# Thirteen buffers in place of ten for a stream of expert weights, a new order of the last chunks, and earlier stores

## The chip, the cores and the metric

The kernel runs on one core of a Trainium2 chip. Its time is the device time of one execution in microseconds (us); of several executions the median is taken. TensorE (PE) multiplies matrices, VectorE (DVE), ScalarE (ACT) and GpSimd (POOL) work element by element, SyncE (SP) here only issues loads and stores, which 16 DMA engines carry out.

## The reference

Two layers of a diffusion transformer act on 256 latent tokens (and, in the first, on 256 context tokens) of width 1024. Layer 0 mixes by neighbourhood attention and a convolution and has a dense feed-forward part. Layer 1 mixes by a state-space model, and its feed-forward part is a mixture of eight experts, each token going to two of them. The change concerns this last part:

```
def moe_swiglu(h, w_router, w1, w3, w2):
    t = h.reshape(-1, shp[-1])
    logits = _f32(t @ w_router)
    top_val, top_idx = lax.top_k(logits, TOP_K)
    top_w = jax.nn.softmax(top_val, axis=-1)
    gate = jnp.einsum('tk,tke->te', top_w, jax.nn.one_hot(top_idx, N_EXPERTS, ...))
    out = gate[:, 0:1] * swiglu(t, w1[0], w3[0], w2[0])
    for e in range(1, N_EXPERTS):
        out = out + gate[:, e:e + 1] * swiglu(t, w1[e], w3[e], w2[e])
```

with `swiglu(h, w1, w3, w2) = (silu(h @ w1) * (h @ w3)) @ w2`, an inner width of 3584, and all weights in 32-bit floating point. The experts' weights are 8 x 3 x 1024 x 3584 numbers, 352 MB, and each is used once. Everything is multiplied in full 32-bit precision or in the three-product split described below.

## The kernel before

**Places for tokens.** After routing, the experts are sorted by how many tokens they got. Eight places are compiled: places 0, 3 and 6 are large, with 128 slots, places 1, 2, 4, 5 and 7 are small, with 64 (`FEW`). Place 0 is always expert 0, so that its weights can be loaded before the routing is known; the others read their expert's number from a register on SyncE (`values_load` in `moe`). If a place overflows, `overflow` runs a slow path behind a test of a counter, which all engines make; with these inputs it isn't taken.

**Chunks and units.** An expert's inner width is cut into seven chunks of 512. A chunk needs six units of weights, each 128 x 2048 numbers, 1 MB: two of w1 (`m1`), two of w3 (`m3`), two of w2 (`m2`). One step of `moe` does the up products of one chunk (`m1`, `m3`) and then the down product (`m2`) of the chunk of the step before.

- A *large* chunk uses units that were split into a high and a low part: ScalarE casts each half of a unit (`wh`, line 203) and VectorE subtracts (`wl`, line 205; GpSimd does it for the names in `ON_POOL`). TensorE then makes three products (`mm3`, lines 223 to 225): 72 matmuls of 512 columns a chunk. A split unit's buffer is free as soon as the split is done. The parts go to a ring of pairs; `need` splits the unit in use and the next two, if they belong to large chunks.
- A *small* chunk uses its units as they are: `up_few` (line 2024) and the small branch of `down` (line 2058), 48 matmuls a chunk, two at a time on two halves of the array. Its buffers are free when the products have read them.

**The ring of loads.** `Stream` keeps a list of free buffers and a list of units in order of use (`mseq`). Every release issues the next unit's load on SyncE's queue, which takes its issues in order; so the order of releases in the program fixes which release a load waits for. The ring has ten buffers in the experts' part: four of its own (`raw`) and six that were lent: one in `xres`, one in `h`, two in `U`, two in `room`. The queue also keeps no more than eight loads under way.

**The pairs.** In the experts' part there are six pairs of split halves: four of the ring (`wh`, `wl`) and two in a tile `more`. During the routing (the end of `s5`) the first three units of expert 0 are split ahead, the third by VectorE (first half) and GpSimd (second half).

**The order of the steps.** `moe_plan` puts three large chunks first and then mixes the other 18 large with the 35 small ones in proportion. Its last steps are the small chunks 4 and 5 of place 7, the last large chunk, the last small chunk. TensorE, ScalarE, GpSimd and SyncE run in the order in which the code is written; VectorE's order is chosen by the scheduler.

**The end.** After an expert's seventh chunk its output is multiplied by the gate of the second residual (`g2row`), scattered back by matmuls with a permutation (`scatter`, `scatter_few`) and added to the residual stream (`added`, line 1923). Each of these six actions of an expert is spread over later steps, one at a time (`ADDS`). At the very end comes the overflow test and then four stores of the result (`full`, line 2187).

Of the kernel before, what the change touches and what calls it, by code (L numbers as in the profile page):

```python
# [156 lines left out]
class Kernel:  # L157
# [1077 lines left out]
    def s5(self, xT):  # L1235
# [218 lines left out]
        gate, self.g2row = gates[:, 0], gates[:, 1]  # L1454
        self.kept(0, gate)
# [118 lines left out]
        first = self.mseq[:3]  # L1574
# [37 lines left out]
        self.split(first[2])  # L1612
# [8 lines left out]
        room = up.tile([P, 2, UNIT], F32, name="room", tag="y")  # L1621
        self.st.lend(room[:, 0], room[:, 1])
# [345 lines left out]
    def moe_plan(self):  # L1968

        many, few = ([(e, c) for e in range(8) if FEW[e] == i for c in range(7)] for i in range(2))  # L1970
        self.steps = many[:LAG]
        del many[:LAG]
        while many or few:
            self.steps.append((many if len(many) * 7 * sum(FEW) > len(few) * (7 * (8 - sum(FEW)) - LAG) else few).pop(0))
        seq, last = [], []
        for e, c in self.steps:
            seq += [(k, e, c, j) for j in range(2) for k in ("m1", "m3")] if FEW[e] else \
                   [(k, e, c, j) for k in ("m1", "m3") for j in range(2)]
            seq += last
            last = [("m2", e, c, j) for j in range(2)]  # L1980
        seq += last
        for s in seq:
            self.st.add(s, partial(self.moe_src, *s))
        self.mseq = seq
        self.expert = {}
# [7 lines left out]
    def moe(self):  # L1993
# [4 lines left out]
        def need(name):  # L1998
            i = pos[name]
            for j in (i, i + 1, i + 2):  # L2000
                if j < len(seq) and not FEW[seq[j][1]]:
                    self.split(seq[j])
# [67 lines left out]
        few = self.hT.rearrange("p k t -> p (k t)")[:, 0:1024].rearrange("p (a b) -> p a b", a=2)  # L2070
# [8 lines left out]
        def finish(e, c, t):  # L2079
# [3 lines left out]
            if c == 6:  # L2083
# [3 lines left out]
                adds.extend([acts[i] for i in v] for v in ADDS)  # L2087
# [45 lines left out]
        while adds:  # L2133
            step()

    def overflow(self):
# [3 lines left out]
        with tc.If(most > 0):  # L2140
            for e in range(8):
                n = nc.values_load(self.cnt[0:1, e:e + 1], min_val=0, max_val=256)
                with tc.If(n > 0):
# [34 lines left out]
                    for n in range(2):  # L2178
                        ready(n)
                        add(n)  # L2180

    def full(self):
        self.layer0()
        for n in range(2):
            for t in range(2):
                s = slice(n * 512, n * 512 + 512)
                self.nc.sync.dma_start(self.out[0, t * P:(t + 1) * P, s], self.x[:, 2 + t, s])
# [100 lines left out]
ADDS = ((0,), (1,), (2,), (3,), (4,), (5,))  # L2288
TAIL = (0, 0, 2, 0, 1, 1)
# [7 lines left out]
LAG = 3  # L2297

# [29 lines left out]
```

## Time and profile before

| what | us |
|---|---|
| median of 3 executions | 1849.68 (1848.10 to 1851.54) |
| profiled execution, its time | 1849.28 |
| profiled execution, its span (first to last instruction) | 1847.5 |
| TensorE busy in the span | 1690.4 (91%) |
| VectorE, ScalarE, GpSimd busy | 1144.5, 719.8, 475.3 |
| loads and stores in the span | 517.03 MB |
| mean granted TensorE clock | 0.962 of 2.4 GHz |

The busy shares are averages over many stages with different limits; a change to one stage is read from that stage. Times in the trace count from the start of the span. TensorE's matmuls overlap, and their ends are modelled, so a busy TensorE is not one at its peak. The DMA share is the mean busy share of the 16 DMA engines (values a little over 1 are rounding of the recorder), GB/s what they moved. "PEclk" is the clock granted to TensorE, as a share of the full 2.4 GHz; 0.50 is the lower level of 1.2 GHz.

### The profile page before, as it was taken

Reading aid. Unit: us, or ns where it says so; the run is one execution under the profiler, and the core shown is the slowest. Engines: PE = TensorE matmul, PEld = TensorE weight load, DVE = VectorE, ACT = ScalarE, POOL = GpSimd, SP = SyncE. Lnnn points to the kernel's source line nnn. Section 1 sums busy time; section 2 is a strip of 40 time slices with the busy share of each in tenths; the row PEclk is TensorE's granted clock in tenths of the full one; section 3 lists DMA queues with packets and bytes.
Section 4 is the critical chain, followed back from the end, with each engine's and each line's share of the span. In section 5 each row is a group of like instructions: output and inputs, shape, how many; then the busy total and the mean of one; then the engine's idle time right before and its main releaser. Section 6 shows DMA issues by size and latency. Waiting matters only on the chain.

```text
span 1847.5 us, 23203 instructions
## 1 busy us (share of the span) xinstructions
PE 1690.4 (91%) x8562; PEld 1122.3 (61%) x8562; DVE 1144.5 (62%) x1614; ACT 719.8 (39%) x1069; POOL 475.3 (26%) x541
## 2 busy tenths in 40 slices
PE   6967899998988999998689999989999999999997
PEld 4855366876766778665567755544544564554553
DVE  4999788577576664669969654454444444445444
ACT  3435563432332332457265533333333332333331
POOL 2347038396695720152432000000000000000000
PEclk9988899999999999999698999999999998999999
DMA  8320743664653653357966899999999999999995
GB/s 320 126 83 23 245 154 139 211 217 145 226 177 119 215 185 114 144 179 142 290 275 232 327 421 420 419 420 420 419 420 420 420 419 398 404 419 421 419 420 225
DMA packets 107432, 517.03 MB, mean 280 GB/s; under 512 B 13792, under 2 KB 41696, under 8 KB 48688
## 3 DMA queue, kind: packets, MB, share of 16 engines
q1 hardware_dynamic: 76672, 490.77, 69.0%
q10 hardware_dynamic: 29968, 22.57, 3.8%
q0 software_dynamic: 672, 2.14, 0.4%
q8 instruction: 69, 1.13, 0.2%
q14 instruction: 51, 0.42, 0.1%
HBM read 496.46 MB, written 18.97 MB: 279 GB/s over the span
## 4 chain that ended last, share of the span: by engine, by line
PE 43%; DMA 12%; DVE 7%; POOL 2%; ACT 1%; issue 1%; SPq 0%; ACTq 0%; DVEq 0%; POOLq 0%
PE m L2024 10%; PE y L2058 5%; DMA U<-in_moe 4%; PE m L223 3%; PE m L224 3%; PE m L225 3%; DMA room<-in_moe 3%; PE w L223 2%; PE w L225 2%; PE w L224 2%; DMA raw<-in_moe 2%; PE y L224 2%; PE y L223 2%; PE y L225 2%; DVE wl L205 1%
## 5 line engine op out<-in xcount | busy, mean ns | idle before, releaser
L205 DVE TENSOR_TENSOR wl<-raw,wh 128x1024 fp32r<-128x1024 f32 x151 | 192.4, 1309 | 93.2 <-ACT wh L203 93.2
L203 ACT CAST wh<-raw 128x1024 fp32r<-128x1024 f32 x172 | 173.6, 1048 | 172.2 <-PE w L225 73.9
L2024 PE MATMUL m<-raw,E 128*64 128x512 f32 x456 | 178.2, 597 | 0.0
L224 PE MATMUL w<-hl,wh 128*128 128x512 f32 (+1 forms) x384 | 143.6, 374 | 1.2 <-POOL hl L568 0.6
L223 PE MATMUL w<-hh,wh 128*128 128x512 f32 (+1 forms) x384 | 144.4, 377 | 0.0
L225 PE MATMUL w<-hh,wl 128*128 128x512 f32 (+1 forms) x384 | 142.4, 372 | 0.0
L1845 POOL TENSOR_SCALAR brow<-order 128x128 fp32r<-128x128 f32 x10 | 9.3, 941 | 473.9 <-PE bk L1880 462.4
L224 PE MATMUL m<-wl,small 128*128 128x512 f32 x252 | 100.9, 401 | 9.7 <-DVE wl L205 9.7
L223 PE MATMUL m<-wh,small 128*128 128x512 f32 x252 | 101.6, 403 | 4.8 <-ACT wh L203 4.8
L2024 PE MATMUL m<-U,E 128*64 128x512 f32 x232 | 105.4, 597 | 0.0
L225 PE MATMUL m<-wh,small 128*128 128x512 f32 x252 | 100.0, 397 | 0.0
L2046 ACT CAST small<-gT 128x512 fp32r<-128x512 f32 x21 | 12.3, 586 | 221.8 <-PE gT L2043 221.8
L2047 DVE TENSOR_TENSOR small<-gT,small 128x512 fp32r<-128x512 f32 x21 | 14.5, 692 | 131.8 <-ACT small L2046 131.8
L2024 PE MATMUL m<-room,E 128*64 128x512 f32 x208 | 94.4, 597 | 0.0
L2024 PEld LDWEIGHTS m<-raw,E 128*64 128x64 f32 x456 | 51.1, 136 | 60.9 <-issue 58.6
L223 PEld LDWEIGHTS w<-hh,wh 128*128 128x128 f32 x384 | 72.2, 188 | 16.7 <-issue 3.6
L224 PEld LDWEIGHTS w<-hl,wh 128*128 128x128 f32 x384 | 72.3, 188 | 14.8 <-POOL hl L568 2.8
L224 PE MATMUL w<-wl,gh 128*128 128x512 f32 x176 | 71.8, 408 | 10.4 <-DVE wl L205 10.4
L225 PEld LDWEIGHTS w<-hh,wl 128*128 128x128 f32 x384 | 72.2, 188 | 12.9
L205 POOL TENSOR_TENSOR wl<-raw,wh 128x1024 fp32r<-128x1024 f32 x21 | 52.7, 2521 | 98.0 <-ACT wh L203 98.0
L2040 ACT COPY E<-gT 128x256 f32<-128x256 f32 x35 | 13.0, 371 | 160.1 <-PE gT L2038 160.1
L223 PE MATMUL w<-wh,gh 128*128 128x512 f32 x176 | 71.6, 407 | 1.9 <-ACT wh L203 1.9
(444 smaller groups left out, 4270.6 us busy)
## 6 DMA issues: line engine op xcount, KB each, us to landing
raw<-in_moe SPq DMA_DIRECT2D x135, 1024.0 KB, 15.5
U<-in_moe SPq DMA_DIRECT2D x67, 1024.0 KB, 15.6
room<-in_moe SPq DMA_DIRECT2D x66, 1024.0 KB, 13.1
raw<-in_ada_w SPq DMA_DIRECT2D x48, 1024.0 KB, 5.3
xres<-in_moe SPq DMA_DIRECT2D x34, 1024.0 KB, 16.4
h<-in_moe SPq DMA_DIRECT2D x34, 1024.0 KB, 17.1
raw<-in_ffn_w SPq DMA_DIRECT2D x30, 1024.0 KB, 5.1
raw<-in_mix_w_in SPq DMA_DIRECT2D x10, 1024.0 KB, 6.5
```

The costliest lines, as they stand in the source:

```text
L203: nc.scalar.copy(wh[:, :m], flat[:, h:h + m])
L205: eng.tensor_tensor(wl[:, :m], flat[:, h:h + m], wh[:, :m].bitcast(F32), op=OP.subtract)
L223: nc.tensor.matmul(o, lhsT=ah, rhs=bh, start=start, stop=False)
L224: nc.tensor.matmul(o, lhsT=ah, rhs=bl, start=False, stop=False)
L225: nc.tensor.matmul(o, lhsT=al, rhs=bh, start=False, stop=stop)
L1845: eng.tensor_scalar(self.perm[:, int(FEW[e]), t], self.iota64 if FEW[e] and not beyond else self.iota, pos, mask, op0=OP.is_equal, op1=OP. ...
L2024: nc.tensor.matmul(o[64 * i:64 * i + 64], lhsT=self.few[:, 4 * j + k], rhs=w[i][:, k], start=not j and not k, stop=j == 1 and k == 3, tile ...
L2040: nc.scalar.copy(gT, pt[:, 0:256])
L2046: nc.scalar.copy(gh, v)
L2047: nc.vector.tensor_tensor(gl, v, gh.bitcast(F32), op=OP.subtract)
L2058: nc.tensor.matmul(y[64 * n:64 * n + 64], lhsT=t[:, 2 * j + f], rhs=w[:, f, n * 512:n * 512 + 512], start=not c and not j and not f, stop= ...
```

## The change

- The ring has 13 buffers, not 10. New are the tile `E[0]` (which held the transposed tokens for routing and then the small experts' inputs and hidden values) and two units in a new tile `more`, in the place of the two split pairs. The small experts' inputs and hidden values move to the tile of the first residual's gate, which is spent by then (`self.spent`).
- Four split pairs remain, so `need` splits the unit in use and only the next one, and the routing splits two units ahead, not three; the third is split in the first step of the experts.
- The order of steps ends with four small chunks: the last three (`LAST`) are kept back when large and small ones are mixed.
- A small expert's six actions at its end are taken in three steps (`FEW_ADDS`).
- The four stores are issued straight after the last addition, ahead of the overflow test; the overflow path stores again if it runs.

```diff
+        self.spent = gate
...
-        first = self.mseq[:3]
+        first = self.mseq[:2]
         self.split(first[0])
...
-        self.split(first[2])
...
         room = up.tile([P, 2, UNIT], F32, name="room", tag="y")
         self.st.lend(room[:, 0], room[:, 1])
+        self.st.lend(E[0].rearrange("p a b c -> p (a b c)"))
+        self.rings = [self.ring_pair]
+        room = up.tile([P, 2, UNIT], F32, name="more", tag="L1")
+        self.st.lend(room[:, 0], room[:, 1])
...
+        n, m = len(many), len(few) - LAST
         while many or few:
-            self.steps.append((many if len(many) * 7 * sum(FEW) > len(few) * (7 * (8 - sum(FEW)) - LAG) else few).pop(0))
+            self.steps.append((many if many and len(many) * m > (len(few) - LAST) * n else few).pop(0))
...
-            for j in (i, i + 1, i + 2):
+            for j in (i, i + 1):
                 if j < len(seq) and not FEW[seq[j][1]]:
                     self.split(seq[j])
...
-        few = self.hT.rearrange("p k t -> p (k t)")[:, 0:1024].rearrange("p (a b) -> p a b", a=2)
+        few = self.spent.rearrange("p (a b) -> p a b", a=2)
...
-                adds.extend([acts[i] for i in v] for v in ADDS)
+                adds.extend([acts[i] for i in v] for v in (FEW_ADDS if FEW[e] else ADDS))
...
         while adds:
             step()
+        self.store()
+
+    def store(self):
+        for t in range(2):
+            for n in range(2):
+                s = slice(n * 512, n * 512 + 512)
+                self.nc.sync.dma_start(self.out[0, t * P:(t + 1) * P, s], self.x[:, 2 + t, s])
...
                     for n in range(2):
                         ready(n)
                         add(n)
+            self.store()
 
     def full(self):
         self.layer0()
-        for n in range(2):
-            for t in range(2):
-                s = slice(n * 512, n * 512 + 512)
-                self.nc.sync.dma_start(self.out[0, t * P:(t + 1) * P, s], self.x[:, 2 + t, s])
...
+FEW_ADDS = ((0, 1), (2, 4), (3, 5))
...
+LAST = 3
```

The order of the steps (L a large chunk, s a small one) was

`L L L s L s L s s L s s L s s L s s L s s L s s L s s L s s L s s L s s L s s L s s L s s L s s L s s L s`

and is now

`L L L s L s L s s L s s L s s L s L s s L s s L s s L s s L s L s s L s s L s s L s L s s L s s L s s L s s s s`

Three places in the engines' orders follow. First SyncE's queue at the end of the routing; the loads are named by the buffer that they fill, and `TENSOR_LOAD cnt` reads the first expert's number. Before:

```order
L85 DMA raw<-in_moe 128x2048 x2
L85 DMA xres<-in_moe 128x2048
L85 DMA raw<-in_moe 128x2048
L85 DMA room<-in_moe 128x2048 x2
L85 DMA h_7842<-in_moe 128x2048
L2104 TENSOR_LOAD cnt
```

The same place in the changed kernel:

```order
L85 DMA raw<-in_moe 128x2048 x2
L85 DMA xres<-in_moe 128x2048
L85 DMA room<-in_moe 128x2048 x2
L85 DMA E_7049<-in_moe 128x2048
L85 DMA more<-in_moe 128x2048 x2
L85 DMA raw<-in_moe 128x2048
L2109 TENSOR_LOAD cnt
```

Two loads more stand ahead of the numbers' reading, and the load into a `raw` buffer that waited for the third split now stands behind the lent tiles.

Second, VectorE at the same place (the names: `pw` holds the routing's small tables, `brow` the selection matrix of the first place, `h` the tokens that are selected). Before, from the ranks of the second half of the tokens on:

```order
L1766 TENSOR_REDUCE pw<-gt 128x8
L1767 TENSOR_SCALAR pw<-pw 128x8
L205 TENSOR_TENSOR more<-raw,more 128x1024
L1752 SCALAR_TENSOR_TENSOR h_7842<-T_7536,rn 128x512 x2
L1781 COPY pw<-pos 128x8
```

and in the changed kernel:

```order
L1770 TENSOR_REDUCE pw<-gt 128x8
L1771 TENSOR_SCALAR pw<-pw 128x8
L1756 SCALAR_TENSOR_TENSOR h_7842<-T_7536,rn 128x512 x2
L1785 COPY pw<-pos 128x8
L1795 TENSOR_SCALAR pw<-pw 128x16
```

The split's subtraction (line 205) has left this place; it stands in the first step of the experts.

Third, VectorE at the end of the program (`m` is a chunk's hidden part, `y` an expert's output, `sc` a scattered part, `xres` the residual). Before:

```order
L2047 TENSOR_TENSOR small<-gT,small 128x512
L205 TENSOR_TENSOR wl<-room,wh 128x1024 x2
L205 TENSOR_TENSOR more<-raw,more 128x1024 x2
L1964 SCALAR_TENSOR_TENSOR gt<-lth,m_12871 64x512
L1908 TENSOR_TENSOR gt<-y,gate_7392 128x512
L1965 SCALAR_TENSOR_TENSOR gt<-gt,m_12871 64x512
L1910 TENSOR_TENSOR adsb<-gt,adsb 128x512
L1908 TENSOR_TENSOR gt<-y,gate_7392 128x512
L1910 TENSOR_TENSOR ntmp<-gt,ntmp 128x512
L1923 SCALAR_TENSOR_TENSOR xres<-sc,order,xres 128x512 x4
L1935 TENSOR_TENSOR adsb<-y,gate_7392 64x512 x2
L1923 SCALAR_TENSOR_TENSOR xres<-sc,order,xres 128x512 x4
```

and in the changed kernel:

```order
L1914 TENSOR_TENSOR ntmp<-gt,ntmp 128x512
L1927 SCALAR_TENSOR_TENSOR xres<-sc,order,xres 128x512
L1968 SCALAR_TENSOR_TENSOR gt<-lth,m_12962 64x512
L1969 SCALAR_TENSOR_TENSOR gt<-gt,m_12962 64x512
L1927 SCALAR_TENSOR_TENSOR xres<-sc,order,xres 128x512 x3
L1968 SCALAR_TENSOR_TENSOR gt<-lth,m_13020 64x512
L1969 SCALAR_TENSOR_TENSOR gt<-gt,m_13020 64x512
L1968 SCALAR_TENSOR_TENSOR gt<-lth,m_13066 64x512
L1969 SCALAR_TENSOR_TENSOR gt<-gt,m_13066 64x512
L1939 TENSOR_TENSOR adsb<-y,gate_7392 64x512 x2
L1927 SCALAR_TENSOR_TENSOR xres<-sc,order,xres 128x512 x4
```

The large place's last splits and its four additions no longer stand behind the last small chunk's hidden part; three small chunks' hidden parts stand behind them.

## Rows read from the trace of the kernel before

**Rows 1.** The page's head.
```profile
span 1847.5 us, 23203 instructions
```

**Rows 2.** Windows: length, engines' busy time, granted clock, DMA share, GB/s.
```profile
960.00:990.00 30.00, 25.56 (x129) 22.51 (x128) 25.27 (x56) 12.20 (x20) 11.12 (x7) 0.77 0.42 163
990.00:1035.00 45.00, 45.00 (x220) 37.83 (x219) 38.49 (x55) 29.52 (x34) 3.08 (x2) 1.00 0.86 331
1035.00:1041.50 6.50, 6.50 (x32) 3.24 (x30) 0.00 (x0) 0.00 (x0) 0.00 (x0) 1.00 0.03 11
1041.50:1540.00 498.50, 482.53 (x2205) 268.05 (x2204) 242.65 (x255) 181.19 (x228) 11.29 (x10) 0.99 1.01 418
1540.00:1590.00 50.00, 48.45 (x201) 25.15 (x200) 23.81 (x26) 14.36 (x18) 0.00 (x0) 0.97 0.96 384
1590.00:1820.00 230.00, 224.07 (x1008) 118.07 (x1006) 99.80 (x104) 76.28 (x97) 1.57 (x2) 1.00 1.01 420
...
989.15:1839.85 850.70, 822.24 (x3722) 461.30 (x3721) 420.43 (x461) 306.59 (x383) 15.94 (x14) 0.99 0.97 401
```

**Rows 3.** Timeline of SyncE's queue, 1030 to 1046: start, length, load.
```profile
1041.14 0.34 SPq L85 DMA_DIRECT2D U<-in_moe  x1
```

**Rows 4.** Chain of waits, 977 to 990: start, length, what.
```profile
978.46 2.33 DVE brow L1845
...
980.84 2.08 PE xT L1851 x8
982.91 0.93 PE pos L1777 x4
983.85 1.91 PE xT L1851 x8
...
985.76 3.63 PE xT L1851 x16
```

**Rows 5.** Timelines of GpSimd and VectorE at the same place.
```profile
978.36 2.34 POOL L205 TENSOR_TENSOR more<-raw,more 128x1024 fp32r<-128x1024 f32 x1
...
982.68 1.22 DVE L205 TENSOR_TENSOR more<-raw,more 128x1024 fp32r<-128x1024 f32 x1
...
985.36 0.34 DVE L1845 TENSOR_SCALAR brow<-pw 128x128 fp32r<-128x128 f32 x1
```

**Rows 6.** Timeline of TensorE where experts change; in brackets the wait before.
```profile
1212.34 0.50 PE L224 MATMUL m<-wl,small 128*128 128x512 f32 x1 [2.94 <-DVE wl L205]
...
1529.16 0.79 PE L224 MATMUL m<-wl,small 128*128 128x512 f32 x1 [2.94 <-DVE wl L205]
...
1689.46 0.50 PE L224 MATMUL y<-wl,small 128*128 128x512 f32 x1 [1.54 <-DVE wl L205]
```

**Rows 7.** Windows of 5 us where the granted clock fell.
```profile
1530.00:1535.00 5.00, 5.00 (x13) 3.83 (x13) 4.79 (x5) 1.79 (x2) 0.00 (x0) 0.50 1.01 418
...
1560.00:1565.00 5.00, 5.00 (x18) 4.03 (x18) 3.42 (x4) 0.00 (x0) 0.00 (x0) 0.75 0.82 326
```

**Rows 8.** Chain of waits: 16 small matmuls, one large, one cast.
```profile
1675.24 3.58 PE y L2058 x16
...
1818.58 1.05 ACT wh L203
...
1822.59 0.23 PE y L225
```

**Rows 9.** The end: a window, then timelines of TensorE, VectorE and SyncE's queue.
```profile
1824.00:1825.00 1.00, 1.00 (x6) 0.81 (x6) 0.97 (x2) 0.00 (x0) 0.00 (x0) 1.00 0.20 82
...
1829.82 1.89 PE L2058 MATMUL y<-U,E 128*64 128x512 f32 x8
...
1835.04 1.40 DVE L1935 TENSOR_TENSOR adsb<-y,gate 64x512 f32<-64x512 f32 x2
1836.93 2.92 DVE L1923 SCALAR_TENSOR_TENSOR xres<-sc,order,xres 128x512 f32<-128x512 f32 x4 [0.49 <-PE sc L1941]
1842.07 2.18 SPq L2187 DMA_DIRECT2D out<-xres  x4
```

## The prediction

> **What bounds the kernel now.** I read the page first, then the windows by stage, then the loading queue, then the chains and waits at the places the change touches. The span is 1847.5 us [rows 1]; the profiled execution took 1849.28 us, so 1.78 us lie outside the span, and the median shown is 1849.68, 0.40 more. The sums below are made against 1849.28.
>
> The experts take 336 units of 1 MB. The windows show the stage that sets the end [rows 2]: from 1041.5 to 1820 us the DMA engines are busy all the time (share 1.01, 418 to 420 GB/s), apart from 1540 to 1590, where they give 384. At 420 GB/s a unit takes 1.0486 MB / 420 GB/s = 2.50 us, and a chunk of six units 15.0 us. Before 1041.5 the DMA engines have time to spare: share 0.42, then 0.86, then 0.03 in the last 6.5 us, because all ten buffers hold units that nobody has finished with. Loading resumes at 1041.14, when expert 1's first two units are consumed [rows 3]. From there to the end the kernel is a queue of loads, and TensorE is not far behind: in the 850.7 us from the first expert matmul to the last addition it is busy 822.2 us [rows 2]. Both must be followed. The last loads land at about 1824.2 (share 0.20 in the slice from 1824 to 1825) [rows 9].
>
> **The change part by part.** I write landing for the time at which the last load is in.
>
> *Three more units in the ring.* At the resumption 16 units are released (12 of the first three chunks' up matrices, 4 of the first two's down matrices), so 16 + 10 = 26 are loaded, and nothing moves. With 13 buffers 29 are. The spare share before (58% of 30 us, 14% of 45, 97% of 6.5: 30 us in all) is enough for 3 x 2.5 = 7.5 us more loading, and the lent tiles are free by then: their last readers (the mixer's last product, the logits) run before the chain of [rows 4] ends. After the resumption the DMA engines are saturated, so the whole lead arrives at the end: **-7.5 us**. Bounds: 0 (the lead is eaten by a later full ring) and -7.5 (no more than three units).
>
> *One split fewer before the experts.* The third unit is no longer split during routing. Its second half on GpSimd takes 978.36 to 980.70, and beside it VectorE's selection matrix (line 1845) takes 2.33 us where the same operation takes 0.34 alone; its first half costs VectorE 1.22 us [rows 4, 5]. On the chain that leads to the first expert matmul the selection becomes 2.0 us shorter, and TensorE's own work behind it (2.08 + 0.93 + 1.91 + 3.63 us) stays; the second selection then is no longer late, since VectorE gains 2.0 + 1.22. So the experts start 2.0 us earlier. The split comes back inside the first chunk: after its pair is free, a cast (1.05) and GpSimd's subtraction (2.34) must end within one unit and a half of matmuls (18 x 0.23 = 4.1 us), which fits with little to spare [rows 5, 8]; I allow one short wait of 0.8, half the shorter waits on a split in [rows 6]. Net **-1.2 us**, because the resumption hangs on this start; bounds -2.0 and +1.
>
> *The dip from 1540 to 1590.* It costs 50 x (420 - 384)/420 = 4.3 us of loading. TensorE had fallen behind there: a wait of 2.94 us on a split at an expert's start, then half clock (granted 0.50 from 1530 to 1535, 0.75 from 1560 to 1565) [rows 2, 6, 7]. Thirteen buffers cover 7.5 us more of such lag: **-4.3 us**; bounds -4.3 and 0.
>
> Landing: 1824.2 - 7.5 - 1.2 - 4.3 = 1811.2.
>
> *Small chunks last.* Now a large chunk's down product and its scatter run behind the landing: 15.65 us from 1824.2 to the last addition at 1839.85 [rows 9]. With four small chunks last, what is left is the second half of the last down product (8 matmuls, 1.89), a hand-over (0.1) and the small scatter from its first product with the gate to its last addition (1835.04 to 1839.85, 4.81): 6.8 us. Difference **-8.85 us**. The large scatter moves in front of the last chunks, beside loading. Bounds: -8.85, and -2 if TensorE lags there. The grouping of a small expert's six scatter actions in three steps moves instructions by single steps and adds none: 0.
>
> *Stores ahead of the test.* Now 7.65 us pass from the last addition to the end of the span. The stores start 2.22 us after it, behind the test; four issues in 2.18 us, so the last begins at 1843.92, and the span ends 3.58 us later [rows 9]. With SyncE waiting at the stores, three of them go out between the additions and the last about 0.1 us after the last addition: 3.7 us. **-3.95 us**. What SyncE now reaches later, the test, waits for nobody's data and its 2.2 us fit beside the last store's way. Bounds: -3.95, and -1.7 if the test's 2.2 us come after the stores.
>
> *TensorE's account.* Small chunks cost TensorE 3 x 3.58 us and four short transposes, 11.2, large ones 72 x 0.23 and four longer ones, 17, both against 15.0 of loading [rows 8]. The 18 remaining large chunks stand among 32 small ones now, not 35, so TensorE gains on the loads more slowly, and recovers the rest in the last chunks. Pure work is 822.2 less about 5 us that the half clock added (0.50 x 5 + 0.25 x 5 = 3.8 in the two windows of [rows 7], the rest beside them and in a third drop near 1478) = 817. It cannot start before 989.15 - 1.2 = 988.0. Six waits on splits at the expert changes (the first and the fourth 2.94, the last 1.54, 12.1 in all) [rows 6] come from VectorE's order, not from loads, and I let them stay, as I do the 5 us. 988.0 + 817 + 12.1 + 5 = 1822.1, against 1811.2 + 6.8 = 1818.0 by the loads. The 4.1 us too many are partly waits for loads by another name; I take half, **+2.0 us**; bounds 0 and +6.
>
> Sum: -7.5 - 1.2 - 4.3 - 8.85 - 3.95 + 2.0 = -23.8, and 1849.28 - 23.8 = **1825.5 us**.
>
> **Rivals.** *The clock drops in the last chunks.* The last four chunks keep TensorE busy 11.2 of every 15 us, with waits for units between bursts. The granted clock falls to the lower level, 1.2 GHz, after the wait of 2.94 us that ends at 1529.16 [rows 6, 7]; but the same wait of 2.94 that ends at 1212.34 left it at 2.4. At 1.2 GHz a small chunk takes 2 x 10.7 + 0.5 = 22 us, 7 more than its loads; two such chunks at the end give +14: 1839.5; one, 1832.5. The Trainium skill speaks against this end of the order: its page "TensorE: Matmul & The Clock Gate", section "HAM oscillation — how this bites in real kernels", says that a loop whose bursts of matmuls are shorter than the wait for the next operand goes back to the slow clock at each of them. By that rule all four chunks would run slow; the trace's two waits of 2.94 us went both ways. I give this 0.15.
>
> *The ring fills and buys nothing.* If TensorE stays behind by a full ring, the loads wait for buffers as at 1035 to 1041.5 [rows 2], now with 13, and the lead of 7.5 and the 4.3 of the dip are both lost: 1825.5 + 11.8 = 1837.3; with the dip alone kept 1829.8. For it: the denser large chunks. Against: share 1.01 with ten buffers from 1041.5 to 1540. This is also the case in which the change doesn't do what it says. 0.12.
>
> *Slower: the split pairs.* With four pairs, not six, a pair comes round once in four halves, 4 x 6 x 0.23 = 5.5 us of matmuls. It is held for 1.4 (matmuls), 1.05 (cast) and 1.22 (subtraction) [rows 5, 8], so 1.8 us remain for queueing on ScalarE and VectorE. Each of the 21 large chunks has 12 halves, 252 in all; to end above 1853, 28 us over the forecast, each must lose 0.11 us, that is, an average of 1.8 + 4 x 0.11 = 2.3 us in those queues. For it: VectorE's other work for a large chunk (three operations of 0.7) stands in that queue. Against: it stands there once in 12 halves. Price 1853 to 1860; 0.06, of which a third ends within 0.2% of before.
>
> *All goes better*: no wait in the first chunk, no surplus on TensorE, and fewer waits at the expert changes: 1818 to 1822. 0.06.
>
> **How the numbers follow.** The forecast has 0.61. Its own range is 1822 (the 2.0 surplus and the 0.8 gone, with rounding) to 1830 (dip kept). The range over the cases reaches from 1820 to 1836, which leaves out most of the clock rival, the end of the full-ring rival and the slower one. A measurement of this kernel can tell about 0.2%, 3.7 us: faster by more 0.94, within 0.02, slower 0.04.
>
> **What would show it.** Right: DMA share near 0 just before a resumption near 1040, then 1.01 without a dip to about 1811; six to eight us from the landing to the last addition; stores issued during the last additions, the span's end under 4 us behind. Wrong: DMA share under 1 after 1045 (full ring); granted clock 0.50 in the last 50 us; TensorE waits on line 205 inside large chunks, not only at expert changes (pairs); a first expert matmul that doesn't come near 987.

## The result and the profile after

The changed kernel took 1828.97 us (median of 4 runs, 1827.09 to 1830.97), the kernel before 1848.89 beside it (4 runs, 1845.15 to 1851.54): ratio 0.9893 with an interval of 0.9879 to 0.9907. The profiled execution took 1829.19 us, 20.1 less than the 1849.28 that the prediction's sum started from; the forecast was 23.8 less. Run again beside e9 and e10, the changed kernel took 1828.57 (e11).

The page's head, to be held against [rows 1]:

```profile
span 1827.4 us, 23220 instructions
...
PE 1679.9 (92%) x8562; PEld 1113.5 (61%) x8562; DVE 1145.8 (63%) x1614; ACT 720.0 (39%) x1069; POOL 469.2 (26%) x541
```

The windows by stage (length, busy time of PE, PEld, DVE, ACT and POOL, granted clock, DMA share, GB/s) answer to [rows 2]:

```profile
985.00:1000.00 15.00, 14.47 (x64) 11.35 (x63) 14.37 (x31) 10.84 (x13) 3.99 (x3) 1.00 0.55 217
...
1030.00:1040.00 10.00, 9.83 (x44) 5.49 (x43) 3.64 (x4) 2.97 (x4) 0.00 (x0) 1.00 0.62 224
1040.00:1050.00 10.00, 9.59 (x42) 5.28 (x40) 8.48 (x9) 7.03 (x9) 0.00 (x0) 1.00 0.92 338
...
1540.00:1590.00 50.00, 50.00 (x221) 28.07 (x221) 26.98 (x28) 18.93 (x24) 0.00 (x0) 0.97 1.01 420
...
1780.00:1800.00 20.00, 18.38 (x74) 6.17 (x72) 4.32 (x7) 0.96 (x2) 0.00 (x0) 1.00 1.01 420
...
1805.00:1810.00 5.00, 5.00 (x25) 1.98 (x23) 1.37 (x2) 0.59 (x1) 0.00 (x0) 1.00 0.86 356
1810.00:1811.00 1.00, 1.00 (x6) 0.24 (x2) 0.00 (x0) 0.00 (x0) 0.00 (x0) 1.00 0.57 238
1811.00:1812.00 1.00, 0.57 (x5) 0.32 (x4) 0.00 (x0) 0.37 (x1) 0.00 (x0) 1.00 0.53 221
1812.00:1813.00 1.00, 0.97 (x6) 0.40 (x8) 0.00 (x0) 0.00 (x0) 0.00 (x0) 1.00 0.26 107
1813.00:1814.00 1.00, 0.97 (x6) 0.09 (x2) 0.00 (x0) 0.00 (x0) 0.00 (x0) 1.00 0.06 25
```

The queue of loads is now full from 1050 to 1805, the dip from 1540 to 1590 included. In the last chunks the clock stays at 1.00, the level of 2.4 GHz. The loads end more slowly than before: the share fades over some 6 us, where it took 3 in the kernel before. The 16 DMA engines finish apart: the trace's records have 16 packets under way until 1807, 9 at 1811 and 3 at 1813.

The end of the chain of waits (start, length, what) shows what sets the end:

```profile
1774.27 19.80 DMA more<-in_moe
1794.19 19.80 DMA raw<-in_moe
1814.03 1.96 PE y L2063 x8
1816.75 1.14 PE sc L1945 x2
1817.91 2.15 DVE xres L1927 x3
```

From 1693.77 on the chain is one load behind another up to 1814, then the last half of a small down product, its scatter and the additions. Against [rows 9]: the large product and its scatter are gone from behind the landing.

SyncE's queue at the end, as a timeline row and then two rows of its waits (us in total, times, longest):

```profile
1818.69 2.69 SPq L2146 DMA_DIRECT2D out<-xres  x4
...
SPq L2152 <- SPq L2152: 2.7, 1, 2.7
SPq L2334 <- PEq L2334: 0.7, 2, 0.5
```

The stores leave between the additions, as the change means them to. But the last addition ends at 1820.71 (start 1817.91 plus 2.80 for four), and the span at 1827.4: 6.7 us, where it was 7.65. Line 2152 is the overflow test. The instructions of that line, for ScalarE and SyncE (durations in ns, then first and last start in us), show where the 2.7 us lie:

```profile
L2152 SPq EVENT_SEMAPHORE  x9: 17/17/17, 1825.1 to 1825.8; - x9
...
L2152 ACTq EVENT_SEMAPHORE  x2: 17/17/17, 1814.7 to 1814.7; - x2
...
L2152 ACTq COMPARE_BRANCH  x1: 58/58/58, 1812.2 to 1812.2; - x1
...
L2152 SPq COMPARE_BRANCH  x1: 53/53/53, 1822.4 to 1822.4; - x1
```

Each engine pauses between its branch and its next instruction: SyncE 2.7 us, ScalarE 2.5, TensorE 3.4, VectorE 3.5, GpSimd 1.0. Only SyncE has issued stores, so its pause need not be a wait for them.

### The profile page after: what moved, and what is told of

Its sections match the earlier page's. It is cut to its first block, busy times and chain, and to the rows that moved or that the text cites. A ratio compares the mean times of both kernels' runs of the same rounds, so it can differ in the third digit from the quotient of the medians.

```text
span 1827.4 us, 23220 instructions
## 1 busy us (share of the span) xinstructions
PE 1679.9 (92%) x8562; PEld 1113.5 (61%) x8562; DVE 1145.8 (63%) x1614; ACT 720.0 (39%) x1069; POOL 469.2 (26%) x541
## 4 chain that ended last, share of the span: by engine, by line
PE 46%; DMA 7%; DVE 7%; ACT 3%; issue 1%; POOL 0%; DVEq 0%; SPq 0%; ACTq 0%; POOLq 0%
PE m L2029 11%; PE y L2063 6%; PE m L223 4%; PE m L224 4%; PE m L225 4%; DMA raw<-in_moe 3%; PE w L223 2%; PE w L224 2%; PE w L225 2%; DMA more<-in_moe 2%; PE y L224 2%; PE y L223 2%; PE y L225 2%; DVE wl L205 1%; DMA U<-in_moe 1%
## 5 line engine op out<-in xcount | busy, mean ns | idle before, releaser
L2029 PE MATMUL m<-raw,gate 128*64 128x512 f32 x384 | 165.7, 597 | 0.4 <-DMA raw<-in_moe 0.4
L224 PE MATMUL m<-wl,small 128*128 128x512 f32 x336 | 134.4, 400 | 13.0 <-DVE wl L205 13.0
L223 PE MATMUL m<-wh,small 128*128 128x512 f32 x336 | 136.4, 406 | 0.0
L225 PE MATMUL m<-wh,small 128*128 128x512 f32 x336 | 133.2, 396 | 0.0
L205 DVE TENSOR_TENSOR wl<-U,wh 128x1024 fp32r<-128x1024 f32 x51 | 62.8, 1265 | 35.9 <-ACT wh L203 35.5
L2029 PE MATMUL m<-more,gate 128*64 128x512 f32 x184 | 83.6, 597 | 1.2 <-DMA more<-in_moe 1.2
L224 PEld LDWEIGHTS m<-wl,small 128*128 128x128 f32 x336 | 64.3, 191 | 30.2 <-DVE wl L205 17.4
L2029 PEld LDWEIGHTS m<-raw,gate 128*64 128x64 f32 x384 | 47.0, 136 | 54.3 <-issue 51.0
L2029 PE MATMUL m<-U,gate 128*64 128x512 f32 x176 | 80.0, 596 | 0.0
```

Of the source, the lines that this page charges most:

```text
L205: eng.tensor_tensor(wl[:, :m], flat[:, h:h + m], wh[:, :m].bitcast(F32), op=OP.subtract)
L223: nc.tensor.matmul(o, lhsT=ah, rhs=bh, start=start, stop=False)
L224: nc.tensor.matmul(o, lhsT=ah, rhs=bl, start=False, stop=False)
L225: nc.tensor.matmul(o, lhsT=al, rhs=bh, start=False, stop=stop)
L2029: nc.tensor.matmul(o[64 * i:64 * i + 64], lhsT=self.few[:, 4 * j + k], rhs=w[i][:, k], start=not j and not k, stop=j == 1 and k == 3, tile ...
```

## How the runs are compared

The first 950 us, which no edit touches, vary by 8 us from one execution to the next. So besides the whole time I measure from a marker in S5 (the state-space stage, ahead of the experts), the first matmul of the last S5 weight whose split lies in the ring's own pairs. Here is that row in the changed kernel; in the profiled execution of before it starts at 951.50:

```profile
950.11 0.39 PE L223 MATMUL so<-wh,yhl 128*128 128x512 f32 x1
```

*First matmul* is the experts' first, *landing* the end of the last half microsecond ahead of the stores in which the DMA share is over 0.1 (so it is known to half a microsecond), *last addition* the end of the last row on `xres`, *end* the rest of the span. The expectations take the landing as the end of the last load in the chain, 0.5 to 0.9 us later. All in us, one profiled execution each; the changed kernel's experts were executed in four of them (changed, e5, e11, and e4 with one register load among them), and marker to last addition came to 870.6, 871.4, 871.1 and 870.6: a spread of 0.8. The experts of the kernel before were executed in two (before and e3), and there it differs by 2.5.

| kernel | marker to first matmul | first matmul to landing | landing to last addition | marker to last addition | end | median of runs |
|---|---|---|---|---|---|---|
| before | 37.65 | 835.9 | 14.9 | 888.35 | 7.65 | 1848.1 to 1849.1 in five sets |
| changed | 35.24 | 828.1 | 7.3 | 870.60 | 6.69 | 1828.97 |
| e1: 10 units | 35.67 | 836.8 | 7.7 | 880.12 | 6.84 | 1839.06 |
| e2: old order | 35.02 | 827.9 | 16.6 | 879.51 | 6.44 | 1837.88 |
| e3: before, stores first | 37.09 | 833.2 | 15.5 | 885.83 | 6.50 | 1845.72 |
| e4: early count | 35.09 | 828.0 | 7.6 | 870.63 | 6.42 | 1829.36 |
| e5: no test | 35.55 | 827.9 | 7.9 | 871.36 | 3.12 | 1825.71 |
| e6: 6 pairs, 11 units | 38.55 | 830.6 | 7.3 | 876.40 | 6.73 | 1834.93 |
| e7: 6 pairs, 10 units | 38.87 | 836.3 | 7.6 | 882.78 | 7.43 | 1839.67 |
| e8: two large first | 34.98 | 827.4 | 7.2 | 869.64 | 7.27 | 1830.48 |
| e9: old order, 10 units | 35.07 | 836.7 | 15.7 | 887.45 | 7.33 | 1847.45 |
| e10: two first, loads as for three | 34.98 | 827.0 | 7.3 | 869.29 | 6.71 | 1826.18 |
| e11: changed, again | 35.54 | 828.2 | 7.4 | 871.09 | 6.64 | 1828.57 |
| e12: mix | 34.94 | 826.1 | 8.3 | 869.32 | 5.68 | 1825.91 |

## The experiments

### e1 and e9: the ring

```
-        self.st.lend(E[0].rearrange("p a b c -> p (a b c)"))
         self.rings = [self.ring_pair]
-        room = up.tile([P, 2, UNIT], F32, name="more", tag="L1")
-        self.st.lend(room[:, 0], room[:, 1])
```

> The changed kernel with the ring at 10 units again: the spent tile E[0] and the two units of L1 are not lent; everything else of the change stays (4 split pairs, the new order, the stores). Theory (the prediction's term): the ring's three more units were transfers ahead of the experts' time, 2.5 us each at the 419 GB/s of the experts' stage, so this comes out 7.5 us above the changed kernel, 1836.5, and up to 11.8 us above it (1841) if the stretch in which the DMA share fell below 1.0 comes back as well. Rival (the ring fills and buys nothing, TensorE sets the end): within 1.5 us of the changed kernel's 1829.

Measured 1839.06, 10 above the changed kernel, and 9.5 from the marker to the last addition. The ring's three units are worth what the prediction gave them and some more; the rival that they buy nothing falls. Of the 9.5, 1.9 is not the lead: from 1060 to 1800 us e1 loses 2.7 us of loading, by the GB/s of windows of 20 us against 420, and the changed kernel 0.8. Where they are missed stands in the windows of e1: the share is lower in the stretch in which the ring stands full ahead of the experts' first releases.

```profile
985.00:1000.00 15.00, 14.47 (x70) 11.75 (x69) 13.26 (x38) 9.13 (x11) 4.00 (x3) 0.95 0.20 71
```

e9 undoes the order as well (the same edit, and the old rule of e2):

> The changed kernel with both the ring of 10 units (4 pairs) and the old rule for the order: the fourth corner beside the changed kernel and the two runs that undid one of the two. Measured from the first matmul of the last S5 weight that lies in the ring's own pairs to the last addition into the result, the other three took 870.6 (changed), 880.1 (ring 10) and 879.5 (old order). Theory (the two terms add up): 889. Rival (they overlap: with 10 units the new order costs the loads some of what it saves behind them, so that the old order is less bad there): 884.5 to 886.5, last landing 5 us earlier than with the ring of 10 and the new order.

Measured 887.45: between the sum and the overlap, 1.6 under the one and 0.9 over the other's range. The landing came only 0.7 us earlier after the marker than in e1 (871.8 against 872.5), not 5, which speaks against the overlap. So the four corners (870.6, 880.1, 879.5, 887.5) give 9.5 and 7.9 for the ring, 8.9 and 7.3 for the order. In e9's windows the dip at 1540 is there again, with the clock at 1.00:

```profile
1540.00:1560.00 20.00, 18.29 (x80) 7.59 (x79) 8.22 (x12) 5.10 (x7) 0.00 (x0) 1.00 0.96 399
1560.00:1580.00 20.00, 20.00 (x90) 10.54 (x91) 11.56 (x12) 6.78 (x8) 0.00 (x0) 1.00 0.96 388
```

That is 20 x (21 + 32)/420 = 2.5 us of loading lost. With 13 units and the same order (e2) the share there is 1.01: the longer ring covers it, as the prediction said. With 10 units and the new order the share there is 1.01 too, but it falls elsewhere: in e1 to 0.97 from 1260 to 1280, in e7 to 0.88 from 1240 to 1260.

The whole time of e9 prices the rest of the change, above all one split fewer and the earlier stores, for which the prediction had -1.2 and -3.95 us. It is 1847.45 against 1848.64 for the kernel before, ratio 0.9998 with an interval of 0.9987 to 1.0008: no difference that the runs can tell.

### e2: the order

```
-        n, m = len(many), len(few) - LAST
         while many or few:
-            self.steps.append((many if many and len(many) * m > (len(few) - LAST) * n else few).pop(0))
+            self.steps.append((many if len(many) * 7 * sum(FEW) > len(few) * (7 * (8 - sum(FEW)) - LAG) else few).pop(0))
```

> The changed kernel with the old rule for the order of the steps, so the small (64-slot) chunks no longer stand last together; ring, pairs and stores as changed. Theory (the prediction's term): from the last load's landing to the last addition it takes 15.65 us again, where the changed kernel took 6.7, with the last landing where it is now (1814): 8.9 us more, 1838. Rival (part of the old tail lay beside the landing of loads that now end unevenly on the 16 DMA engines, so the order gave less): 4 to 6 us more, 1833 to 1835.

Measured 1837.88, 8.9 above the changed kernel, and 8.9 from the marker to the last addition, all of it behind the landing. At the end of e2's chain of waits a large chunk's last splits and its place's four additions (1824.43) stand ahead of the small scatter again:

```profile
1814.70 2.37 DVE wl L205 x2
1820.07 3.65 PE y L2062 x16
1824.43 2.72 DVE xres L1927 x4
1827.80 4.09 PE sc L1945 x8
1831.91 0.75 DVE xres L1927
```

The theory holds; the rival of 4 to 6 us falls.

### e3: the stores alone, in the kernel before

```
         while adds:
             step()
+        self.store()
```

(and the four stores taken out behind the test, put in again at the end of its body)

> The kernel before with one edit: the four stores of the result are issued ahead of the overflow test (and again within it, if it is taken). The prediction's term was 3.95 us, so 1845.0. Theory now, from the changed kernel's trace: SyncE goes through the test behind the stores, and the span ends 6.7 us after the last addition where it ended 7.65 after it: 0.95 us less, 1848. Rival: the wait for the stores' landing and the test's end add up in full, nothing gained, 1848.9.

Measured 1845.72, ratio 0.9994 to before with an interval of 0.9983 to 1.0006: no difference that the runs can tell. In the trace the end takes 6.50 us, not 7.65: 1.15 less. That excludes 3.95.

This trace tells of the dip, too. Its experts are those of the kernel before, word for word, yet the marker to the last addition is 2.5 us shorter. In the place of [rows 7] its windows read:

```profile
1530.00:1535.00 5.00, 5.00 (x25) 3.86 (x24) 4.58 (x6) 1.93 (x3) 0.00 (x0) 1.00 1.01 419
1550.00:1560.00 10.00, 8.29 (x31) 4.89 (x28) 6.66 (x7) 2.14 (x3) 0.00 (x0) 1.00 0.98 403
1560.00:1570.00 10.00, 10.00 (x42) 3.16 (x41) 1.50 (x2) 4.20 (x6) 0.00 (x0) 1.00 1.00 403
```

The row of the wait ahead of it, as in [rows 6], is the same 2.94 us:

```profile
1527.12 0.50 PE L224 MATMUL m<-wl,small 128*128 128x512 f32 x1 [2.94 <-DVE wl L205]
```

The clock did not fall, and the dip costs 20 x 17/420 = 0.8 us, not 4.3. Three executions with 10 units and the old order lost 4.3, 2.5 and 0.8 us there, the largest beside half clock.

### e4 and e5: the test behind the stores

e4 loads the count early; the branch on it stays:

```
+            if i == 20:
+                self.most = nc.values_load(self.cnt[0:1, 8:9], min_val=0, max_val=256)
...
-        most = nc.values_load(self.cnt[0:1, 8:9], min_val=0, max_val=256)
-        with tc.If(most > 0):
+        with tc.If(self.most > 0):
```

> The changed kernel with the count that the overflow test looks at loaded into each engine's register in step 20 of the experts instead of at the test; the test itself stays behind the stores. Theory (the register's load is most of what SyncE does behind the stores): the span ends 4 to 5 us after the last addition in place of 6.7, 1827. Rival (what counts is the wait for the stores' landing where the test's two ways meet, and the branch behind it): no change, 1829 within 0.5.

Measured 1829.36; the end takes 6.42 us, 0.27 less and hardly under the shortest of the ten executions that have the stores and the whole test in this order (6.44 to 7.43). SyncE reaches the branch 0.5 us after the last addition, where it took 1.7, but the pause behind it is 3.4 us in place of 2.7. e5 calls no `overflow` at all:

```
                 self.moe()
-                self.overflow()
```

> The changed kernel without the overflow path and without the test ahead of it (that part of the computation is left out; with this input no slot overflows). It prices the test behind the stores. Theory: without it the span ends about 4.7 us after the last addition (one issue 0.67, a landing of 2.7 as in the kernel before, 1.3 behind that), where the changed kernel took 6.7: 2.0 us less, 1827 against 1829. Rival (the test runs beside the stores' landing and costs nothing): still 6.5 to 6.8 after the last addition.

Measured 1825.71 (ratio to before 0.9869 to 0.9903), the end takes 3.12 us. So the test behind the stores costs 6.69 - 3.12 = 3.6 us, more than the 2.0 of the theory and more than the 2.2 that stand between the last addition and the stores in the kernel before [rows 9]. Those 2.2 us were not SyncE's way through the test, as rows of the kernel before show (the instructions of the test's line, and a row of SyncE's waits):

```profile
L2140 DVEq EVENT_SEMAPHORE  x2: 21/21/21, 1842.0 to 1842.1; - x2
...
L2140 SPq COMPARE_BRANCH  x1: 53/53/53, 1806.8 to 1806.8; - x1
...
L2140 DVEq COMPARE_BRANCH  x1: 72/72/72, 1839.1 to 1839.1; - x1
```

```profile
SPq L2187 <- DVEq L2140: 15.6, 1, 15.6
```

SyncE had branched at 1806.8; the stores waited for VectorE, which branched at 1839.1, beside its last addition, and went on at 1842.0. In the changed kernel SyncE itself goes through the test behind the stores, from 1821.4 to 1825.8. SyncE's waits at the end, of e4 and then of e5:

```profile
SPq L2153 <- SPq L2153: 3.6, 2, 3.4
```

```profile
SPq L2333 <- DMA out<-xres: 1.3, 2, 0.7
```

Without the test SyncE waits for the stores' landing; with it, it pauses behind the branch. In the changed kernel a store lands 3.2 us after its issue, the last one by that at about 1824.2 (an estimate), ahead of SyncE's next instruction at 1825.1. The DMA queues of the changed kernel in its last 3.1 us (packets, MB, share) show one small packet of the stores' queue and two that bring instructions; e5 has none of the latter in its last 11 us:

```profile
q14 instruction: 2, 0.02, 1.5%
q1 hardware_dynamic: 1, 0.00, 0.1%
```

That the engines fetch code there is in the rows; that this is what the pause behind a branch consists of is likely, and not shown.

### e6 and e7: two pairs against two units

e7 has the old ring and the old pairs under the new order, e6 the same with `E[0]` lent:

```
-        self.rings = [self.ring_pair]
-        room = up.tile([P, 2, UNIT], F32, name="more", tag="L1")
-        self.st.lend(room[:, 0], room[:, 1])
...
-            for j in (i, i + 1):
+            for j in (i, i + 1, i + 2):
```

> The changed kernel with the old 10 units and the old 6 pairs (look-ahead of two units), so that the new order, the stores and the later third split are all that is left of the change. Against the run with 10 units and 4 pairs (1839.1) it shows what two pairs are worth alone, measured from the experts' first matmul to the last landing, which took 837.7 us there. Theory (pairs cost next to nothing): 836.5 to 838. Rival (two pairs fewer cost 2.5 us and more): 835 and less.

> The changed kernel with L1 left to the split pairs: 6 pairs and a look-ahead of two units as before, the ring at 11 units (E[0] still lent). It weighs two pairs against two units. Theory (units are worth 2.5 us each and the pairs little): 5 us above the changed kernel, 1834, first matmul of the experts to last landing 833.6 us where the changed kernel took 828.6. Rival (the four pairs leave waits that cost 3 us): 1831. Rival (the pairs are worth more than the units): below 1829.

e7 took 1839.67, as long as e1 (1839.06). From the first matmul to the landing, counted as the expectation does, it is 837.2 (the last load of its chain ends at 1822.05), inside the theory: 0.5 us less with the two pairs. That is not the price of the pairs alone, since e7 loses 3.9 us of loading from 1220 to 1260, where its clock fell to 0.50 (1210 to 1215), and e1 only 1.6 at such a place. The pairs cost more than 0.5 at the start, as the look-ahead of two asks for the third split ahead of the first matmul, 3.2 us later than in e1. Over both, 882.8 against 880.1: with six pairs it is 2.7 longer. e6 took 1834.93, near the theory's time, but not on its way: counted as there, its loads take 831.1 us from the first matmul and not 833.6, and the first matmul comes 3.3 later. From the first matmul to the last addition the eleventh unit gives 6.1 us (843.9 in e7 to 837.9), the twelfth and thirteenth, with two pairs fewer, 2.5 (to 835.4). Of the 6.1, 3.7 is loading that e7 lost between 1060 and 1800 us and e6 didn't. So a unit brings its 2.5 us of lead, or less, and more where the longer ring bridges a stretch in which TensorE falls behind.

### e8, e10 and e12: a version that loads sooner

What is left in the queue is the share missing from 985 to 1050. e8 puts two large chunks first (`LAG = 2`) and holds loads until SyncE has the experts' numbers:

```
-        while self.free and self.at < len(self.specs):
+        while self.free and self.at < min(len(self.specs), self.limit):
...
-LAG = 3
+LAG = 2
```

> The changed kernel with two chunks of 128 slots ahead of the first small one where it had three; loads of other experts are held until SyncE has their numbers, so 10 units are issued ahead of that and not 15. Theory (the loads that are missing from 985 to 1060 us, some 13 us of the queue's time, are missing because large chunks free units more slowly than they load): with the third large chunk later the ring frees sooner, first matmul to last landing falls by 2.5 to 5 us from 828.6, total 1824 to 1827. Rival (the five units held back are missed in full): 1829 to 1841, with the DMA share in 985 to 1000 below 0.55.

Measured 1830.48, marker to last addition 869.64. The rival's time came, and its share below 0.55 in the first stretch. Of the theory came that the pause at 1030 goes, but first matmul to landing is only 0.7 us shorter.

```profile
985.00:1000.00 15.00, 14.45 (x73) 11.76 (x72) 13.92 (x43) 9.25 (x12) 4.02 (x3) 0.99 0.31 114
...
1030.00:1040.00 10.00, 9.58 (x41) 7.25 (x40) 9.59 (x10) 7.63 (x8) 0.00 (x0) 1.00 1.01 420
```

e10 loads in the order for three and computes in the order for two (`s = self.steps`):

```
+        for steps in (s[0:2] + [s[3], s[2]] + s[4:], s):
```

> As the run with two large chunks ahead of the first small one, but the loads keep the order in which three would go first: expert 0's third chunk is loaded ahead of the first small chunk and used behind it, so nothing is held back for the experts' numbers. Theory (that run gave back in 985 to 1000 us, DMA share 0.31, what it won from 1030 to 1050, 1.01): with both the share is 0.5 or more in the first stretch and 0.9 or more from 1000 on; 2 to 4 us below the changed kernel, 1825 to 1827. Rival (units that lie longer in the ring make it smaller: the share falls below 0.8 in 1010 to 1050): 1829 and no gain.

Measured 1826.18 (1824.31 to 1828.67), 2.4 below the changed kernel's 1828.57 beside it, and 869.29 from the marker: 1.3 to 2.1 less. The first stretch is filled, and the rival's pause is there, only earlier:

```profile
985.00:1000.00 15.00, 14.45 (x63) 11.35 (x62) 14.58 (x24) 10.38 (x12) 4.13 (x3) 1.00 0.62 228
...
1010.00:1020.00 10.00, 9.83 (x44) 5.45 (x42) 3.64 (x4) 2.91 (x4) 0.00 (x0) 1.00 0.46 176
```

e12 loads only two units ahead of their turn, and moves the stores to ScalarE's queue:

```
+        third = [("m1", 0, 2, j) for j in range(2)]
+        loads = [s for s in seq if s not in third]
+        loads[10:10] = third
...
-                self.nc.sync.dma_start(self.out[0, t * P:(t + 1) * P, s], self.x[:, 2 + t, s])
+                self.nc.scalar.dma_start(self.out[0, t * P:(t + 1) * P, s], self.x[:, 2 + t, s])
```

> Two edits in two places that don't touch, read apart in the trace. (a) Two large chunks ahead of the first small one, the first two units of expert 0's third chunk loaded ahead of it, the rest in the order of use; 12 units are issued ahead of the experts' numbers. Theory (between the run that held back five units and the one that held back none): DMA share 0.4 to 0.5 from 985 to 1000 and 0.95 or more from there on, 868 to 869.3 from the marker in S5 to the last addition, where the changed kernel took 870.9. Rival: a pause as in 1010 to 1020 of the run that held none back (0.46), over 869.5. (b) The four stores are issued by ScalarE's queue and not SyncE's, so that SyncE reaches the test's end ahead of them. Theory (SyncE's way through the test stands on the path only since it comes behind its own issues): the span ends 4 to 5.5 us after the last addition, in place of 6.7. Rival (what counts is what follows the landing, on whatever engine): 6.4 to 6.8 still. In all 1824 to 1826, or 1826 to 1828 by the second rival alone.

Measured 1825.91 (1822.50 to 1827.83), ratio to before 0.9862 to 0.9898. (a) The share is better than expected in the first stretch (0.77), a pause of 0.77 remains from 1010 to 1020, and the marker to the last addition is 869.32: just outside the theory's range, no better than e10. (b) The end takes 5.68 us, 1.0 less and a little over the theory's 5.5. SyncE is through its branch at 1788.3 there; ScalarE branches behind the stores (1816.6) and goes on at 1819.4, so the pause of 2.8 us is now on its way. e10 and e12 are the fastest complete versions, 2.4 to 3.1 us under the changed kernel's medians. That is 0.15%, and their intervals to before overlap with its own, so the whole time alone would not prove it. The parts in the trace speak for it, with one execution each: 1.3 us less to the last addition than the lowest of the changed kernel's four, and in e12 an end 0.8 us shorter than the shortest with SyncE's stores ahead of the whole test.

## Why the prediction was right, and where it was wrong

Whole time and sign are right. Against the sum of -23.8 the profiled execution gives -20.1, and it splits like this: 1.4 of gain lies ahead of the marker and is not the change's; marker to landing -10.2 (forecast -13.0); landing to last addition -7.5 (forecast -8.85); the end -0.95 (forecast -3.95); TensorE's surplus 0 (forecast +2.0).

**Three more units, -7.5.** Right in the mean: 9.5 with the new order (e1), 7.9 with the old (e9 to e2). Without the loading that the ten units lost after 1060 (1.9 and 2.5 us more than the thirteen) the lead itself is 7.6 and 5.4. So -7.5 as the outer bound held for the lead, near enough, and not for what the units save in all.

**One split fewer, -1.2.** The start is as forecast, the cost in the first chunk is missized. The two selections on VectorE take 0.35 and 0.34 us now, where the first took 2.33 [rows 4], and the first matmul comes 2.0 to 2.4 sooner after the marker. The slow pair of operations did not vanish. GpSimd's half of a split now falls beside another VectorE operation, behind the first matmul, as the timelines of GpSimd, VectorE and TensorE show:

```profile
977.10 0.35 DVE L1849 TENSOR_SCALAR brow<-pw 128x128 fp32r<-128x128 f32 x1
...
989.88 2.38 DVE L1802 TENSOR_SCALAR pw<-pw 128x2 f32<-128x2 f32 x1
```

```profile
989.83 2.41 POOL L205 TENSOR_TENSOR wl<-raw,wh 128x1024 fp32r<-128x1024 f32 x1 [12.81 <-ACT wh L203]
```

```profile
994.85 0.50 PE L224 MATMUL m<-wl,small 128*128 128x512 f32 x1 [0.53 <-DVE wl L205]
```

The Trainium skill's page "SBUF — State Buffer", section "SBUF: two separate sides", says that GpSimd and certain VectorE operations (in a two-port mode, or with two inputs in SBUF) take a shared pair of ports exclusively, each for a whole instruction. A VectorE operation on 128x2 elements that takes 2.38 us beside a GpSimd operation of 2.41 agrees with it, if the operation is of these kinds, which no run here shows. The one wait of 0.53 on TensorE is below the 0.8 allowed, but TensorE was the wrong place to look: a unit that is split later is freed later. From e3 to e9, which differ in the pairs, this split, the grouping of a small expert's actions and the tile of its inputs, the first matmul comes 2.0 sooner and the landing after it 3.5 later, DMA share 0.22 where it was 0.71 from 985 to 1000:

```profile
985.00:1000.00 15.00, 14.46 (x71) 11.59 (x70) 13.85 (x35) 10.11 (x12) 4.01 (x3) 1.00 0.22 74
```

Net +1.6, or about 0 if the dips of the two are taken out (2.5 against 0.8). The prediction's -1.2 is not seen, but with a spread of 2.5 between before and e3 the size stays open.

**The dip, -4.3.** The cure was right (1.01 with 13 units), the size was that of one execution with half clock; two others lost 0.8 and 2.5. With the ring, 11.8 us were forecast and 7.9 to 9.5 measured.

**Landing, in all.** 2.8 us fell short. The fading end is in no term of the sum: in windows of half a microsecond the share leaves out 2.7 us of loading in the changed kernel's last 6 us up to the landing, and 1.5 in the last 3 us of the kernel before, 1.2 us more. The split's term missed by 1.2 or more. How the shortfall divides between these and the dip, single executions don't settle.

**Small chunks last, -8.85.** Right: 8.9 and 7.3 in the two pairs of runs.

**Stores ahead of the test, -3.95: the step that failed.** The prediction took the 2.22 us between the last addition and the stores [rows 9] for SyncE's price of the test, let it fit beside the last store's way, and set a bound of -1.7 in case it came behind. The runs show -0.95 and -1.15, below that bound; against the 6.44 to 7.43 of the ten executions with this end the gain is 0.2 to 1.2. The 2.22 us were what was left of VectorE's way through the test after its last addition. SyncE's own way, from the register's load over the pause behind the branch to the last of its nine semaphore steps, is 4.4 us (1821.4 to 1825.8), longer than a store's 3.2 us to landing, and 1.6 us of the program's end follow. That the test waits for nobody's data was right; its price and the overlap were wrong. In all it costs 3.6 us there (e5). What the change gained is the issues beside the additions, 5.43 - 3.12 = 2.3 us (5.43 is what came from the start of the stores on before: 7.65 - 2.22); what it paid back is 3.6 - 2.2 = 1.4.

**TensorE's surplus, +2.0.** There is none; the last 120 us of the chain up to the landing are loads.

That the profiled time came within 3.7 us of the forecast is in part luck. Without the surplus, which isn't there, the terms make -25.8, and from the marker on the runs show -18.7. The surplus of 2.0 and the 1.4 ahead of the marker hid almost half of the 7.1 between them.

**The rivals.** The clock rival did not come: TensorE waited 1.23 us for a load at 1799.11, was busy 18.38 of 20 us, and kept 1.00. The Trainium skill's section "HAM oscillation — how this bites in real kernels" ("TensorE: Matmul & The Clock Gate") speaks of bursts of matmuls shorter than the wait for the next operand. The prediction applied it to chunks in which, by its own sum, TensorE works 11.2 of every 15 us, where the bursts are the longer part. So it should not have stood against this order, and this trace doesn't test it. The full ring did not come (1.01 from 1050 on). Nor did the split pairs: TensorE's waits for VectorE's splits came to 19.2 us with six pairs (before) and 16.9 with four (changed).

## What to carry to other kernels

In a stage that is a queue of loads, count when each buffer is freed and not only when the consumer waits: a split moved behind the first matmul shows almost no wait on TensorE (0.53 us) and still thins out the loads behind it (a share of 0.22 where it was 0.71). Price a test at the end of a program by leaving it out once; moved behind the stores it may cost more than it did ahead of them. Every engine goes through the test, so look which one was on the way before and which one is after. When the start of a stage varies by more than the effect, compare from a marker inside the trace: here executions of the same experts agreed within 0.8 us for the changed kernel and 2.5 for the kernel before, where the start alone varied by 8.

## What the hardware showed unexpectedly

The 16 DMA engines, all busy at 420 GB/s up to about 1805, did not end together. The share was under 0.9 without a break for 6.0 us before the landing in the changed kernel, 4.5 in e1, 5.0 in e2, and 3.0 in the kernel before. Why it differs is open; no run was made for it. Every engine pauses behind the branch of the overflow test, from 1.0 us (GpSimd) to 3.5 (VectorE) in the changed kernel, although only SyncE issues stores there. And after the same wait of 2.94 us, at the same place of the same experts, the clock fell to 0.50 in the kernel before [rows 6, 7] and stayed at 1.00 in e3.
